# Output projection of a hybrid decoder layer as seven block products of half size

## The chip, the cores and the metric

The kernel runs on one core of a Trainium2 chip. The metric is the device time of one execution in microseconds (us). Five engines matter: TensorE (PE), which multiplies; VectorE (DVE) and ScalarE (ACT), which do the element-wise work; GpSimd (POOL), which does almost nothing here; and SyncE (SP), which issues the transfers from memory. Each works through its own queue in order, and a semaphore makes an instruction wait for one on another engine. Matrix products accumulate in PSUM, in banks of 128 x 512 fp32 numbers.

## What is computed

One decoder layer on 512 tokens of width 1024. The part that the change touches:

```
mixed = sigmoid(gate_a) * y_a + sigmoid(gate_b) * y_b     # [512, 1024]
x = x + mixed @ w_out                                     # w_out [1024, 1024]
h = rmsnorm(x, g_ffn)
x = x + (silu(h @ w1) * (h @ w3)) @ w2
```

Before it stand the two token mixers and their projections (y_a, y_b), after it the feed-forward block (FFN), a gated embedding and a last norm. Results are wanted in fp32.

## The kernel before

**Products in three parts.** Every operand of a large product is split into two fp32r numbers, hi and lo: `split` (L74 to L76) casts hi on ACT (L75) and subtracts on DVE to get lo (L76). `mm3` (L88 to L92) then issues three matmuls, hi by hi (L90), and the two mixed ones (L91, L92). The operand that stands in the array takes a weight load, the other streams its columns: 512 of them for a full bank. Below, "a pass" is one DVE instruction over a 128 x 1024 tile.

**w_out.** Mixed comes transposed, features on partitions, as eight k-tiles `mxh`, `mxl` (L816), made in a loop over four pairs b (L817 to L835): two gate products in PSUM (c), a multiplication into the tile GT (L832), a sum (L834), a split (L835). `down_norm` and `down` (L857 to L907) multiply it with w_out: for each of 8 k-tiles, 4 token tiles t and 2 output halves n, one `mm3` into one of eight accumulators that stand in all eight PSUM banks. That is 8 x 4 x 2 x 3 = 192 matmuls of 512 columns. The tokens stand in the array and the rows of w_out stream. Those rows are loaded by `unit` (L284) in the order of the list `order` (L281), 512 KB each, and split by `wunit` (L78). The last three k-tiles (TAIL = 3) go accumulator by accumulator, so that each bank can be read into the residual `xs` (L882, 8 reads of 512 columns) while the next still accumulates.

**Norm.** With both halves of a token tile in `xs`, `norm` (L123 to L133) squares and sums on ACT (L127), scales on DVE (L129), takes the power on POOL (L130) and multiplies on DVE in two halves (L132). `norm_b` (L913) transposes the result on PE (L920, eight 128-column transposes for a token tile) and splits it into `hhi` and `hlo`. Token tiles 0 and 1 are transposed between the last w_out matmuls; then the FFN begins with `proj_b` (`mm<-hhi,w`, 256 columns), and tiles 2 and 3 follow inside it. Its first weights are the split tile `w10`, made by the hook `load_w1`.

**Order.** PE takes its instructions in the order in which the code is written (L304). For the other engines a scheduler lays out one queue each; what stands in them is quoted below from the built programs.

Of the kernel before, what the change touches and what calls it, by code (L numbers as in the profile page):

```python
# [38 lines left out]
def kernel(  # L39
# [139 lines left out]
    for i, (half, src) in ((0, (0, pT)), (1, (0, wpl)), (0, (1, pT)), (2, (0, wpl)), (1, (1, wpl)), (2, (1, wpl))):  # L179
        raw, hi, lo = ups[i]  # L180
# [97 lines left out]
    for b in range(4):  # L278
        for br in range(2):
            order += [wf[28 + 8 * br + 2 * b], wf[28 + 8 * br + 2 * b + 1], wbr[br, b]]  # L280
    order += [wout[k * P:(k + 1) * P, :] for k in range(KC)]  # L281
    loaded = []

    def unit(ahead=2):  # L284
# [523 lines left out]
    def b16(dt, name):  # L808
        return bp.tile([P, 8, T], dt, tag="b16", name=name, bufs=4)
# [118 lines left out]
    def load_w1(k):

        if k == KC - 4:  # L930
            w = b16(F32R, "w10").rearrange("p (u s k) c -> p u s (k c)", u=2, s=2)
            ws.extend(wunit(w1[f], w[:, f, 0], w[:, f, 1]) for f in range(2))
# [42 lines left out]
    wcount = [0]

    def wtile():
        wcount[0] += 1
        if wcount[0] % 5 < 3:
            return [ring.tile([P, 1024], F32R, tag=tg, name=tg) for tg in ("whi", "wlo")]  # L980
        return [bp.tile([P, 1024], F32R, tag=tg, name=tg, bufs=2) for tg in ("g2h", "g2l")]
# [267 lines left out]
```

## Time and profile before

| | us |
|---|---|
| median of 3 runs | 819.32 (819.28 to 820.4) |
| the profiled execution | 821.62 |
| its span in the trace | 819.8 |
| PE busy | 807.1 (98%) |
| DVE busy | 534.4 (65%) |
| first w_out matmul starts | 372.67 |
| first FFN matmul starts | 418.08 |

The profiled execution is 1.82 us longer than its span (what lies ahead of and behind it), and 2.3 us above the median. Starts are counted from the start of the span. A matmul's listed length includes the time until its result is in the bank; matmuls overlap, so the distance of two starts says what one costs the engine. The same holds for DVE.

### The profile page before, as it was taken

The numbers are of one execution on the slowest core, as the hardware profiler recorded it, in microseconds if no ns is written. First come the engines' busy times: TensorE is split into PE (matmuls) and PEld (weight loads), VectorE is DVE, ScalarE is ACT, GpSimd is POOL, SyncE is SP. The second block draws the span as 40 slices with busy tenths as digits, with TensorE's granted clock in tenths as the row PEclk, the third lists the DMA queues.
The fourth block names the chain that finished last, engine by engine and source line by source line (L and its number), as shares of the span: only waits on it lengthen the run. The fifth ranks groups of instructions, "written<-read, shape, count | busy, mean of one in ns | idle before, by whom it ended". The sixth has DMA issues, their size and how long they took to land.

```text
span 819.8 us, 12525 instructions
## 1 busy us (share of the span) xinstructions
PE 807.1 (98%) x4996; PEld 714.5 (87%) x4996; DVE 534.4 (65%) x879; ACT 365.7 (45%) x679; POOL 42.3 (5%) x67
## 2 busy tenths in 40 slices
PE   8999999999999999999999999999999999999996
PEld 6798888888788888888899999999999988888885
DVE  4878699847673334423489998888887433446654
ACT  6557434435552322322366555555555333434332
POOL 2021100111200000000000000000000000000000
PEclk8999999999999999999999999999999999999999
DMA  8434333211035332233441323333334522443121
GB/s 333 164 97 138 104 101 102 83 52 52 28 108 200 103 102 89 92 103 103 158 163 48 135 92 104 105 109 108 108 111 149 213 84 98 145 163 103 40 89 53
DMA packets 35803, 92.82 MB, mean 113 GB/s; under 512 B 7448, under 2 KB 12184, under 8 KB 35744
## 3 DMA queue, kind: packets, MB, share of 16 engines
q1 hardware_dynamic: 35744, 92.02, 34.3%
q8 instruction: 39, 0.64, 0.3%
q14 instruction: 20, 0.16, 0.1%
HBM read 85.17 MB, written 6.83 MB: 112 GB/s over the span
## 4 chain that ended last, share of the span: by engine, by line
PE 92%; DVE 2%; issue 1%; ACT 1%; POOL 1%; POOLq 0%; DVEq 0%; ACTq 0%
PE c L90 17%; PE c L92 17%; PE c L91 17%; PE mm L90 11%; PE mm L91 11%; PE mm L92 11%; PE c L270 3%; PE pc L90 1%; PE pc L91 1%; PE pc L92 1%; PE c L274 1%; PE c L920 0%; ACT scr L756 0%; POOL fm L120 0%; DVE r L610 0%
## 5 line engine op out<-in xcount | busy, mean ns | idle before, releaser
L76 DVE TENSOR_TENSOR wlo<-raw,whi 128x1024 fp32r<-128x1024 f32 (+1 forms) x102 | 121.3, 1191 | 131.0 <-ACT whi L75 130.3
L75 ACT CAST whi<-raw 128x1024 fp32r<-128x1024 f32 (+1 forms) x102 | 104.4, 1026 | 175.6 <-PE mm L91 66.2
L90 PE MATMUL mm<-hhi,whi 128*128 128x512 f32 x320 | 126.8, 396 | 0.0
L92 PE MATMUL mm<-hhi,wlo 128*128 128x512 f32 x320 | 124.8, 390 | 0.0
L91 PE MATMUL mm<-hlo,whi 128*128 128x512 f32 x320 | 124.7, 390 | 0.0
L92 PEld LDWEIGHTS mm<-hhi,wlo 128*128 128x128 f32 x320 | 60.1, 188 | 12.7
L90 PEld LDWEIGHTS mm<-hhi,whi 128*128 128x128 f32 x320 | 60.1, 188 | 11.8
L91 PEld LDWEIGHTS mm<-hlo,whi 128*128 128x128 f32 x320 | 60.2, 188 | 11.7
L90 PE MATMUL c<-whi,g2h 128*128 128x512 f32 x132 | 51.6, 391 | 0.0
L92 PE MATMUL c<-whi,g2l 128*128 128x512 f32 x132 | 51.4, 389 | 0.0
L91 PE MATMUL c<-wlo,g2h 128*128 128x512 f32 x132 | 51.4, 389 | 0.0
L90 PE MATMUL c<-hhi,whi 128*128 128x256 f32 x168 | 47.7, 284 | 0.0
L91 PE MATMUL c<-hlo,whi 128*128 128x256 f32 x168 | 47.5, 283 | 0.0
L92 PE MATMUL c<-hhi,wlo 128*128 128x256 f32 x168 | 47.5, 283 | 0.0
L75 ACT CAST whi<-sv 128x1024 fp32r<-128x1024 f32 x24 | 25.2, 1052 | 32.5 <-PE pc L91 23.6
L130 POOL TENSOR_TENSOR rstd<-rstd,nhalf 128x1 f32<-128x1 f32 x12 | 6.6, 552 | 554.2 <-DVE rstd L129 554.2
L76 DVE TENSOR_TENSOR g2l<-gg,g2h 128x512 fp32r<-128x512 f32 x22 | 15.0, 688 | 28.2 <-ACT g2h L75 28.2
L91 PEld LDWEIGHTS c<-hlo,whi 128*128 128x128 f32 x168 | 32.2, 192 | 0.0
L92 PEld LDWEIGHTS c<-hhi,wlo 128*128 128x128 f32 x168 | 32.2, 192 | 0.0
L90 PEld LDWEIGHTS c<-hhi,whi 128*128 128x128 f32 x168 | 32.2, 192 | 0.0
L76 DVE TENSOR_TENSOR wlo<-sv,whi 128x1024 fp32r<-128x1024 f32 x24 | 29.1, 1220 | 4.4 <-ACT whi L75 4.4
L75 ACT CAST g2h<-gg 128x512 fp32r<-128x512 f32 x22 | 13.5, 617 | 36.2 <-PE c L91 33.8
(387 smaller groups left out, 2136.1 us busy)
## 6 DMA issues: line engine op xcount, KB each, us to landing
raw<-in_w_dram SPq DMA_DIRECT2D x66, 512.0 KB, 3.5
raw<-in_wf_dram SPq DMA_DIRECT2D x44, 512.0 KB, 3.4
raw<-in_wbr_dram SPq DMA_DIRECT2D x8, 512.0 KB, 3.3
raw<-in_wout_dram SPq DMA_DIRECT2D x8, 512.0 KB, 3.4
raw<-in_wpg_dram SPq DMA_DIRECT2D x8, 512.0 KB, 3.5
gm<-in_x_dram SPq DMA_DIRECT2D x4, 512.0 KB, 8.4
gb<-in_gains_dram SPq DMA_DIRECT2D x4, 512.0 KB, 4.7
pp_dram<-GT SPq DMA_DIRECT2D x8, 256.0 KB, 4.9
```

Source lines behind the costliest of these rows:

```text
L75: S.copy(hi, src)
L76: V.tensor_tensor(lo, src, hi.bitcast(F32), ALU.subtract)
L90: PE.matmul(ps, lhsT=ah, rhs=bh, start=first, stop=False, skip_group_check=more)
L91: PE.matmul(ps, lhsT=ah, rhs=bl, start=False, stop=False, skip_group_check=more)
L92: PE.matmul(ps, lhsT=al, rhs=bh, start=False, stop=last, skip_group_check=more)
L130: G.tensor_tensor(r, r, nhalf[:, 0:1], ALU.pow)
L270: PE.matmul(ps, lhsT=lhsT, rhs=rhs, start=start, stop=stop)
L274: PE.transpose(ps, src, ident if idn is None else idn)
```

## The change

mixed (A) and w_out (B) are cut into 2 x 2 blocks. Token tiles 0 and 1 are the upper half of A, tiles 2 and 3 the lower; of each pair of k-tiles the even one belongs to the left half of A (and the upper of B), the odd one to the right (lower); the output's two halves of 512 columns are the left and right half of B. Seven products of blocks, each of 256 tokens by 512 features by 512 columns, replace the eight of the plain way:

```
P1 = A11 B11   P2 = A12 B21   P3 = S1 T1   P4 = S2 T2
P5 = S4 B22    P6 = S3 T3     P7 = A22 T4
S1 = A21 + A22, S2 = S1 - A11, S3 = A11 - A21, S4 = A12 - S2
T1 = B12 - B11, T2 = B22 - T1, T3 = B22 - B12, T4 = B21 - T2
```

Each product is 2 token tiles (tp) x 4 pairs x 3 = 24 matmuls of 512 columns. A's sums are made by DVE on 256 elements inside the loop over b (L883 to L889), and for each factor of a product there is a split of 128 x 1024 (`s12`, `s43`, `a12`, and two of weights). B's sums are DVE passes of 1024 elements (L1021, L1029, L1042, L1043, two each) in tiles `ra` and `rb`, which hold all of w_out unsplit in the space of `hhi` and `hlo`; so these loads (L858, eight of 512 KB) can start only once the branch products before w_out have read `hhi`. B11 and B21 come by loads of their own (L842, eight of 256 KB) into `raw`.

Of the eight banks the products use six: P1, P4, P6, P7 follow each other in one pair (`pa`, c_3509 and c_3510 below), P3 and P5 in another (`pb_`, mm8_3590 and mm8_3591), and P2 has its own. After each product `res` (L1000) adds each of its two banks to one block of `xs` (14 reads instead of 8), and the next product of the same pair adds on top of what the bank holds. Thus the read of a bank must be over before that bank's next product begins. Token tiles 0 and 1 are normed after P5 and transposed after P6's two halves; tiles 2 and 3 are normed after P7. `load_w1` is called ahead of P6.

```diff
-    order += [wout[k * P:(k + 1) * P, :] for k in range(KC)]
...
-            V.tensor_tensor(tg[j], tg[j], tg[2 + j], ALU.add)
-            split(mxh[:, 2 * b + j, :], mxl[:, 2 * b + j, :], tg[j])
+            V.tensor_tensor(mx[:, b, j, :], tg[j], tg[2 + j], ALU.add)
+        split(a12[:, :, 0, b, :], a12[:, :, 1, b, :], mx[:, b, :, lo_t])
+
+        V.tensor_tensor(s1[:, b, :], mx[:, b, 0, hi_t], mx[:, b, 1, hi_t], ALU.add)
...
+        if b == 3:
+            w_out_first()
...
-    xn = down_norm(KC, lambda k: (mxh[:, k, :], mxl[:, k, :]), load_w1, xs, gb, norm_b)
+    def sprod(acc, tp, pa, pb, first, pairs=range(4)):
+        ah, al = pa
+        c = slice(tp * P, tp * P + P)
+        for i in pairs:
+            mm3(acc, ah[:, i, c], al[:, i, c], *pb[i], first and i == 0, i == 3, not first)
+
+    def res(acc, t, n):
+        c = slice(n * 512, (n + 1) * 512)
+        V.scalar_tensor_tensor(xs[:, t, c], acc, 0.5, xs[:, t, c], ALU.mult, ALU.add)
...
+    for u in us:
+        V.tensor_tensor(ra[:, u, 512:], rb[:, u, 512:], ra[:, u, 512:], ALU.subtract)
+        V.tensor_tensor(rb[:, u, 0:512], rb[:, u, 0:512], ra[:, u, 0:512], ALU.subtract)
+    split(*S3, mx[:, :, 0, hi_t])
+    T3 = bparts(lambda u: ra[:, u:u + 2, 512:])
+    xn = []
+    for tp in range(2):
+        sprod(pb_[tp], tp, S4, B22, False)
+        res(pb_[tp], tp, 1)
+        xn.append(norm(xs[:, tp, :], gb))
+    split(*A11, mx[:, :, 1, hi_t])
+    T4 = bparts(lambda u: rb[:, u:u + 2, 0:512])
+    load_w1()
+    for tp in range(2):
+        sprod(pa[tp], tp, S3, T3, False)
+        res(pa[tp], 2 + tp, 1)
+        norm_b(tp, xn[tp])
+    for tp in range(2):
+        sprod(pa[tp], tp, A11, T4, False)
+        res(pa[tp], 2 + tp, 0)
+        xn.append(norm(xs[:, 2 + tp, :], gb))
```

(`split(*A11, ...)` here writes the block A22 into the tile that held A11.)

**DVE, the end of w_out.** Before, in the last stretch DVE reads accumulators (L882), norms, and splits a few weights:

```order
L76 TENSOR_TENSOR w10_3632<-raw_3637,w10_3632 128x1024
L76 TENSOR_TENSOR wlo_3644<-raw_3641,whi_3643 128x1024
L882 SCALAR_TENSOR_TENSOR xs_3464<-c_3474,xs_3464 128x512
L882 SCALAR_TENSOR_TENSOR xs_3464<-c_3475,xs_3464 128x512
L129 TENSOR_SCALAR rstd_3670<-ss_3668 128x1
L882 SCALAR_TENSOR_TENSOR xs_3464<-c_3476,xs_3464 128x512
L132 SCALAR_TENSOR_TENSOR xn_3667<-xs_3464,rstd_3670,gb_3469 128x512 x2
```

After, between the reads of P4's banks and those of P5's (mm8_3590, mm8_3591) there stand seven passes:

```order
L1000 SCALAR_TENSOR_TENSOR xs_3499<-c_3509,xs_3499 128x512
L1000 SCALAR_TENSOR_TENSOR xs_3499<-c_3510,xs_3499 128x512
L1042 TENSOR_TENSOR ra_3489<-rb_3490,ra_3489 128x2x512
L1043 TENSOR_TENSOR rb_3490<-rb_3490,ra_3489 128x2x512
L1042 TENSOR_TENSOR ra_3489<-rb_3490,ra_3489 128x2x512
L1043 TENSOR_TENSOR rb_3490<-rb_3490,ra_3489 128x2x512
L76 TENSOR_TENSOR s43_3618<-mx_2654,s43_3618 128x1024
L76 TENSOR_TENSOR g2l_3662<-ra_3489,g2h_3661 128x1024
L76 TENSOR_TENSOR g2l_3666<-ra_3489,g2h_3665 128x1024
L1000 SCALAR_TENSOR_TENSOR xs_3499<-mm8_3590,xs_3499 128x512
L1000 SCALAR_TENSOR_TENSOR xs_3499<-mm8_3591,xs_3499 128x512
```

And from there to the read of P6's first bank (c_3509, the last row) five more, with the norms of token tiles 0 and 1 between them:

```order
L76 TENSOR_TENSOR a12_2655<-mx_2654,a12_2655 128x1024
L129 TENSOR_SCALAR rstd_3685<-ss_3683 128x1
L76 TENSOR_TENSOR wlo_3714<-rb_3490,whi_3713 128x1024
L132 SCALAR_TENSOR_TENSOR xn_3682<-xs_3499,rstd_3685,gb_3504 128x512 x2
L129 TENSOR_SCALAR rstd_3706<-ss_3704 128x1
L76 TENSOR_TENSOR wlo_3718<-rb_3490,whi_3717 128x1024
L132 SCALAR_TENSOR_TENSOR xn_3703<-xs_3499,rstd_3706,gb_3504 128x512 x2
L76 TENSOR_TENSOR w10_3721<-raw_3722,w10_3721 128x1024
L76 TENSOR_TENSOR w10_3721<-raw_3726,w10_3721 128x1024
L1000 SCALAR_TENSOR_TENSOR xs_3499<-c_3509,xs_3499 128x512
```

What moved: the splits of `w10` now stand directly ahead of the read of P6's first bank, and the norms' multiplications stand behind P7's weight splits.

**PE, the end of w_out.** Before, transposes of normed tiles stand between matmuls of other accumulators:

```order
L91 MATMUL mm8_3478<-wlo_3644,mxh_2654 128x512
L92 MATMUL mm8_3478<-whi_3643,mxl_2655 128x512
L920 MATMUL c_3713<-cst_sb_75,xn_3667 128x128 x4
L90 MATMUL mm8_3479<-whi_3574,mxh_2654 128x512
L91 MATMUL mm8_3479<-wlo_3575,mxh_2654 128x512
```

There the four transposes of one half of tile 0 (xn_3667) come when five accumulators are done. After, tile 0's (xn_3682) stand between P6's two banks:

```order
L91 MATMUL c_3509<-g2l_3666,s43_3618 128x512
L92 MATMUL c_3509<-g2h_3665,s43_3618 128x512
L976 MATMUL c_3743<-cst_sb_75,xn_3682 128x128 x4
L976 MATMUL c_3751<-cst_sb_75,xn_3682 128x128 x4
L90 MATMUL c_3510<-g2h_3661,s43_3618 128x512
```

and tile 1's (xn_3703) between P6's last matmul and P7's first:

```order
L92 MATMUL c_3510<-g2h_3665,s43_3618 128x512
L976 MATMUL c_3772<-cst_sb_75,xn_3703 128x128 x4
L976 MATMUL c_3780<-cst_sb_75,xn_3703 128x128 x4
L90 MATMUL c_3509<-whi_3713,a12_2655 128x512
L91 MATMUL c_3509<-wlo_3714,a12_2655 128x512
```

What moved: the transposes came from between the products of other accumulators to two places with one product on either side, and P7's first matmul goes to the bank (c_3509) that the last DVE row above reads.

## Rows read from the trace of the kernel before

**Rows 1.** The page: busy time, and busy tenths in 40 slices of the span.
```profile
PE 807.1 (98%) x4996; PEld 714.5 (87%) x4996; DVE 534.4 (65%) x879; ACT 365.7 (45%) x679; POOL 42.3 (5%) x67
...
DVE  4878699847673334423489998888887433446654
...
PEclk8999999999999999999999999999999999999999
```

**Rows 2.** Windows: from:to us, length, busy by engine (instructions), PEclk, DMA share, GB/s.
```profile
5.00:10.00 5.00, 3.41 (x8) 1.94 (x9) 3.45 (x5) 2.75 (x6) 0.00 (x0) 0.73 0.95 349
10.00:15.00 5.00, 5.00 (x15) 3.95 (x14) 1.57 (x3) 2.38 (x5) 0.56 (x1) 0.59 1.03 389
...
405.00:415.00 10.00, 10.00 (x50) 8.26 (x49) 7.00 (x12) 4.75 (x9) 1.12 (x2) 1.00 0.33 137
...
435.00:445.00 10.00, 9.86 (x82) 9.69 (x82) 10.00 (x10) 5.57 (x7) 0.00 (x0) 1.00 0.01 2
```

**Rows 3.** Timeline of PE, before and in the w_out stage: start us, length us, instruction.
```profile
367.01 0.39 PE L92 MATMUL mm<-hhi,wlo 128*128 128x512 f32 x1
...
372.67 0.39 PE L90 MATMUL c<-whi,mxh 128*128 128x512 f32 x1
...
373.35 0.39 PE L90 MATMUL c<-whi,mxh 128*128 128x512 f32 x1
...
418.08 0.28 PE L90 MATMUL mm<-hhi,w 128*128 128x256 f32 x1
```

**Rows 4.** Timeline of DVE, the w_out stage and the FFN's start.
```profile
372.87 0.69 DVE L832 SCALAR_TENSOR_TENSOR GT<-GT,c 128x512 f32<-128x512 f32 x1
...
415.18 0.15 DVE L129 TENSOR_SCALAR rstd<-ss 128x1 f32<-128x1 f32 x1 [0.36 <-ACT xn L127]
415.32 0.69 DVE L882 SCALAR_TENSOR_TENSOR xs<-c,xs 128x512 f32<-128x512 f32 x1
415.99 1.41 DVE L132 SCALAR_TENSOR_TENSOR xn<-xs,rstd,gb 128x512 f32<-128x512 f32 x2
417.32 1.28 DVE L76 TENSOR_TENSOR hlo<-c,hhi 128x512 fp32r<-128x512 f32 x2
418.52 0.68 DVE L882 SCALAR_TENSOR_TENSOR xs<-c,xs 128x512 f32<-128x512 f32 x1
419.12 2.35 DVE L76 TENSOR_TENSOR wlo<-raw,whi 128x1024 fp32r<-128x1024 f32 x2
...
431.93 1.21 DVE L76 TENSOR_TENSOR g2l<-raw,g2h 128x1024 fp32r<-128x1024 f32 x1
433.07 1.22 DVE L961 TENSOR_TENSOR hF<-hF 128x1024 f32<-128x1024 f32 x1
```

**Rows 5.** Groups of DVE by shape, 420 to 640 us; and ACT's casts, on the page.
```profile
L1078 DVE TENSOR_TENSOR GT<-pc,GT 128x256 f32<-128x256 f32 x20 | 8.5, 424 | 12.6 <-PE pc L92 12.4
...
L75 ACT CAST whi<-raw 128x1024 fp32r<-128x1024 f32 (+1 forms) x102 | 104.4, 1026 | 175.6 <-PE mm L91 66.2
```

**Rows 6.** DMA issues: line, KB each, us from issue to landing (the page).
```profile
raw<-in_wout_dram SPq DMA_DIRECT2D x8, 512.0 KB, 3.4
...
gm<-in_x_dram SPq DMA_DIRECT2D x4, 512.0 KB, 8.4
```

**Rows 7.** Timeline of PE near the start: [idle before it, and the releaser].
```profile
5.13 0.50 PE L90 MATMUL mm<-whi 128*128 128x512 f32 x1 [0.49 <-ACT whi L75]
...
7.82 0.79 PE L90 MATMUL mm<-whi 128*128 128x512 f32 x1 [1.23 <-ACT whi L75]
...
9.56 0.63 PE L90 MATMUL mm<-whi 128*128 128x512 f32 x1
9.99 0.63 PE L91 MATMUL mm<-wlo,whi 128*128 128x512 f32 x1
...
14.21 0.39 PE L92 MATMUL mm<-whi,wlo 128*128 128x512 f32 x1
```

**Rows 8.** Timeline of PE at 220 us, a wait inside the kernel.
```profile
219.86 0.63 PE L274 MATMUL c<-cst_sb,num 128*128 128x128 f32 x4 [1.34 <-DVE num L759]
```

More of the change, by code (lines that the diff above doesn't have):

```diff
@@ L813, with wtile, halves, bparts @@
         split(gsh[:, i, :], gsl[:, i, :], gm[:, i, :])
-    mxh, mxl = b16(F32R, "mxh"), b16(F32R, "mxl")
+    wcount = [0]
+    def wtile():
+        wcount[0] += 1
+        if wcount[0] % 5 < 3:
+            return [ring.tile([P, 1024], F32R, tag=tg, name=tg) for tg in ("whi", "wlo")]
+        return [bp.tile([P, 1024], F32R, tag=tg, name=tg, bufs=2) for tg in ("g2h", "g2l")]
+    def halves(t):
+        return t.rearrange("p (u c) -> p u c", c=512)
+    def bparts(src):
+        us = []
+        for u in (0, 2):
+            hi, lo = wtile()
+            split(halves(hi), halves(lo), src(u))
+            us += [(hi[:, c:c + 512], lo[:, c:c + 512]) for c in (0, 512)]
+        return us
+    def from_dram(odd):
+        def src(u):
+            raw = ring.tile([P, 1024], F32, tag="raw", name="raw")
+            for i in range(2):
+                k = 2 * (u + i) + odd
+                nc.sync.dma_start(raw[:, 512 * i:512 * i + 512], wout[k * P:(k + 1) * P, 0:512])
+            return halves(raw)
+        return src
+    bw = {}
+    def w_out_first():
+        wcount[0] = 2
+        bw["B11"] = bparts(from_dram(0))
+        bw["B21"] = bparts(from_dram(1))
+        for n, tg in (("ra", "hhi"), ("rb", "hlo")):
+            bw[n] = hp.tile([P, 4, D], F32, tag=tg, name=n)
+        for n in ("ra", "rb"):
+            for i in range(4):
+                k = 2 * i + (n == "rb")
+                nc.sync.dma_start(bw[n][:, i, :], wout[k * P:(k + 1) * P, :])
+    mx = b16(F32, "mx").rearrange("p (b j) t -> p b j t", j=2)
+    a12 = b16(F32R, "a12").rearrange("p a b -> p (a b)").rearrange("p (j s b t) -> p j s b t", j=2, s=2, t=256)
+    s1 = xnp.tile([P, D], F32, tag="xn", name="s1").rearrange("p (b t) -> p b t", t=256)
+    lo_t, hi_t = slice(0, 256), slice(256, 512)
     for b in range(4):
@@ L833 @@
         for j in range(2):
-            V.tensor_tensor(tg[j], tg[j], tg[2 + j], ALU.add)
-            split(mxh[:, 2 * b + j, :], mxl[:, 2 * b + j, :], tg[j])
+            V.tensor_tensor(mx[:, b, j, :], tg[j], tg[2 + j], ALU.add)
+        split(a12[:, :, 0, b, :], a12[:, :, 1, b, :], mx[:, b, :, lo_t])
+        V.tensor_tensor(s1[:, b, :], mx[:, b, 0, hi_t], mx[:, b, 1, hi_t], ALU.add)
+        V.tensor_tensor(mx[:, b, 0, hi_t], mx[:, b, 0, lo_t], mx[:, b, 0, hi_t], ALU.subtract)
+        V.tensor_tensor(mx[:, b, 0, lo_t], s1[:, b, :], mx[:, b, 0, lo_t], ALU.subtract)
+        V.tensor_tensor(mx[:, b, 1, lo_t], mx[:, b, 1, lo_t], mx[:, b, 0, lo_t], ALU.subtract)
+        if b == 3:
+            w_out_first()
     banks = [0]
@@ L926, with load_w1 @@
     ws = []
[L928 to L932, printed above, removed]
-    xn = down_norm(KC, lambda k: (mxh[:, k, :], mxl[:, k, :]), load_w1, xs, gb, norm_b)
+    def load_w1():
+        w = b16(F32R, "w10").rearrange("p (u s k) c -> p u s (k c)", u=2, s=2)
+        ws.extend(wunit(w1[f], w[:, f, 0], w[:, f, 1]) for f in range(2))
+    def sprod(acc, tp, pa, pb, first, pairs=range(4)):
[3 more added lines that the diff above has]
+            mm3(acc, ah[:, i, c], al[:, i, c], *pb[i], first and i == 0, i == 3, not first)
@@ new lines, in res, with parts4, b16s @@
+    def res(acc, t, n):
+        c = slice(n * 512, (n + 1) * 512)
+        V.scalar_tensor_tensor(xs[:, t, c], acc, 0.5, xs[:, t, c], ALU.mult, ALU.add)
+    def parts4(t, i):
+        return t[:, i, 0], t[:, i, 1]
+    def b16s(name):
+        t = b16(F32R, name).rearrange("p a b -> p (a b)").rearrange("p (j s b t) -> p j s b t", j=2, s=2, t=256)
+        return parts4(t, 0), parts4(t, 1)
+    ra, rb = bw["ra"], bw["rb"]
+    A11, A12 = parts4(a12, 0), parts4(a12, 1)
+    pa = [mm8() for _ in range(2)]
@@ new lines @@
+    for pairs in ((0, 1, 2), (3,)):
+        for tp in range(2):
+            sprod(pa[tp], tp, A11, bw["B11"], True, pairs)
+    for tp in range(2):
+        res(pa[tp], tp, 0)
+    S1, S2 = b16s("s12")
+    split(*S1, s1)
+    us = [slice(u, u + 2) for u in (0, 2)]
+    for u in us:
+        V.tensor_tensor(ra[:, u, 0:512], ra[:, u, 512:], ra[:, u, 0:512], ALU.subtract)
+    T1 = bparts(lambda u: ra[:, u:u + 2, 0:512])
+    pc = [mm8() for _ in range(2)]
+    for tp in range(2):
+        sprod(pc[tp], tp, A12, bw["B21"], True)
+        res(pc[tp], tp, 0)
@@ new lines @@
+    split(*S2, mx[:, :, 0, lo_t])
+    for u in us:
+        V.tensor_tensor(ra[:, u, 0:512], rb[:, u, 512:], ra[:, u, 0:512], ALU.subtract)
+    T2 = bparts(lambda u: ra[:, u:u + 2, 0:512])
+    pb_ = [mm8() for _ in range(2)]
+    for tp in range(2):
+        sprod(pb_[tp], tp, S1, T1, True)
+        res(pb_[tp], 2 + tp, 1)
+    S4, S3 = b16s("s43")
+    split(*S4, mx[:, :, 1, lo_t])
+    B22 = bparts(lambda u: rb[:, u:u + 2, 512:])
+    for tp in range(2):
+        sprod(pa[tp], tp, S2, T2, False)
+        res(pa[tp], tp, 1)
@@ new lines @@
+    for u in us:
+        V.tensor_tensor(ra[:, u, 512:], rb[:, u, 512:], ra[:, u, 512:], ALU.subtract)
[3 more added lines that the diff above has]
+    xn = []
+    for tp in range(2):
+        sprod(pb_[tp], tp, S4, B22, False)
[3 more added lines that the diff above has]
+    T4 = bparts(lambda u: rb[:, u:u + 2, 0:512])
@@ L937 @@
+    load_w1()
+    for tp in range(2):
+        sprod(pa[tp], tp, S3, T3, False)
+        res(pa[tp], 2 + tp, 1)
+        norm_b(tp, xn[tp])
+    for tp in range(2):
+        sprod(pa[tp], tp, A11, T4, False)
+        res(pa[tp], 2 + tp, 0)
+        xn.append(norm(xs[:, 2 + tp, :], gb))
     order += [w3[0], w3[1]]
@@ L974 @@
     raws, parts_ = {}, {}
[L975 to L981, printed above, removed]
+    wcount[0] = 0
     def p_load(j):
```

## Prediction

> **What bounds the kernel now.** The page comes first: PE is busy for 98% of the span and runs at full clock after the first slices, DVE for 65% with much room in the middle [rows 1]. So time comes from PE, and another engine can only take some away. Next the windows of the w_out stage: from 405 to 415 us PE is busy all the time, DVE for 7.00 of 10 us and ACT for 4.75; a little later, from 435 to 445, DVE is busy for the whole 10.00 and PE waits 0.14 [rows 2]. That says two things: nothing holds PE back in w_out, and DVE is not far from being the bound in this part of the kernel. Last, the timelines: the first w_out matmul starts at 372.67, the first FFN matmul at 418.08, which makes the stage 45.41 us long; the first three matmuls, one mm3, take 0.68, hence 0.2267 for one [rows 3]. The 192 matmuls are 43.5 of it, the 16 transposes and their borders the other 1.9.
>
> **What PE saves.** Seven products of 24 matmuls are 168, which is 24 fewer: 24 x 0.2267 = 5.44 us. The 16 transposes stay. Left alone, PE would begin the FFN at 412.6 instead of 418.08.
>
> **What DVE gets.** The path that decides runs over DVE, and I add it up from its own row. The last gate product lands in PSUM and DVE multiplies it at 372.87 [rows 4]; this does not move, since the gate matmuls before it are the same. From there the order after has, up to and including the read of P6's first bank, these instructions, counted row by row:
>
> 25 passes over 1024 elements: 8 sums of weights (L1021, L1029, L1042, L1043), 10 splits of weights (T1, T2, B22, T3 and T4, two each), 5 splits of A's factors (s12 and s43 two each, a12 one), 2 splits of w10. Two of the same kind take 2.35, and from one to the next it is 1.14 (431.93 to 433.07) [rows 4]. 25 x 1.14 = 28.50.
>
> 13 instructions of 512 elements: the gate product itself, one sum, one split, and 10 reads of banks. A read of a bank is followed by the next instruction after 0.60 (418.52 to 419.12) [rows 4]. 13 x 0.60 = 7.80. A 14th, the read of P6's first bank, counts in full: 0.69.
>
> 4 small sums of 256 elements: their length is 0.42 [rows 5]; the next starts 0.08 before the end, as with the others, so 0.34 each, 1.36.
>
> Two norms: 0.14 for the scaling (415.18 to 415.32), 1.33 for the two multiplications (415.99 to 417.32) [rows 4], together 2.94.
>
> The sum is 41.29, so the read ends at 372.87 + 41.29 = 414.16. P7's first matmul adds to the bank just read and cannot start before. A matmul after a wait shows 0.50 against 0.39 [rows 7], so I add 0.11. P7 is 24 x 0.2267 = 5.44, and the FFN begins at 419.71: **1.63 us later than before**. In other words PE could stand at P7 at 407.2, waits 7.0 for DVE in all, and has 5.44 to pay for it.
>
> Does DVE really run without a gap? At each place where it waits for PE I compared both sums. Reading P2's second bank comes at 384.7 by DVE's sum; PE has it at 383.7. P3's banks are read at 387.6 and 390.5; PE has them at 386.4 and 389.2. P4's second bank comes at 395.1, with PE done at 394.9: the closest place, and a wait of a few tenths there would go straight into the result. P5's follow four sums and three splits later, when PE has long stopped.
>
> **Where PE waits.** P6's first matmul with a lo part needs the 19th pass: 402.6 by DVE's sum, 400.1 by PE's. That is 2.5 (P4 may take some tenths of it). Next, the transposes of tile 0 need the first half of xn, which stands behind a split of T3, two reads, the split of A22 and one of T4: 408.0, against PE at 405.1, so 2.9. P7's wait is the rest, about 1.4, since P6's second half and tile 1's transposes fill 408.7 to 412.7. The two w10 splits were spread out before; now they stand right ahead of the read that P7 waits for, and cost 2.28 of the sum.
>
> **What I cost at nothing.** ACT's casts: each is 1.03 [rows 5], shorter than the DVE pass of the same tile; the stage has about 25 of them, some 26 us in 41, and ACT was busy 4.75 in 10 [rows 2]. If a cast is late, DVE stops and the sum grows by as much. The loads: 8 x 256 KB come early, while the branch products run. The 8 x 512 KB wait for the last reader of hhi, which starts at 367.01 and is done at 367.4 [rows 3]. The first sum of weights wants rows 0 and 2 of them, second and third in the queue, at 374.07. One load of 512 KB takes 3.4 [rows 6]; further ones at 389 GB/s [rows 2] 1.35 each: 367.5 + 3.4 + 2.7 = 373.6, so 0.5 to spare. The first read of a bank moves up by the whole stage, and the banks are free, since six of eight are used. Sums that read what the instruction before wrote may wait for its end: 5 such places at 0.08, 0 to 0.4; I take 0. Behind w_out, reads and norms of tiles 2 and 3 stand where they stood; at most the 0.14 of PE's wait at 435 to 445 comes back.
>
> **A rule on DVE against the rows.** In the timeline the next instruction starts 0.08 before the listed end of a pass of 1.22, even where the two have nothing in common (431.93, 433.07) [rows 4]. The Trainium skill, page "VectorE: DVE Perf Modes", section "The DRAIN you can't avoid", says that the next op does not start until the pipe is empty. If so, each instruction costs its listed length. The trace disagrees by these 0.08.
>
> **The rivals.** The base case is the sum: 819.32 + 1.63 = 820.95, so 821.0. The profiled execution of before would become 823.2, as it lies 2.3 above the median.
>
> (a) *The clock falls.* Near the start PE waited 0.49 and 1.23 with three matmuls between; then the windows show a granted clock of 0.73 and 0.59, and a matmul took 0.43 (9.56 to 9.99) until 14.2, that is for 6.4 us [rows 2, 7]. Full speed is 2.4 GHz, the low level 1.2. Against it: a single wait of 1.34 at 219.86 [rows 8] left the clock alone [rows 1]. Here there are 2.5 and 2.9 with one half product between, more than either. If the clock falls behind the second wait, 12 matmuls take 0.20 more each, 2.4, and the transposes about 0.9, less the 1.4 that P7 waits anyway: +1.9. If it has fallen before and recovers by then: 0. If it falls behind the third wait: 15 matmuls of P7, +3.0. I take +1.5: 822.5, with 0 to 3.0.
>
> (b) *The weights come late.* Four loads of 512 KB issued together took 8.4 in the middle [rows 6]. If the third needs that, it lands at 375.9, and everything on DVE shifts by 1.8: 822.8. For it: the queue holds eight such loads. Against it: they have the memory nearly to themselves.
>
> (c) *DVE is not the bound.* If its chain is short enough, because sums and splits on strided halves take less than the rows I took, or overlap more, the 24 matmuls show: 819.32 - 5.44 = 813.9. It decides at a chain of 39.7 us for no change and at about 34.3 for the whole gain. Passes would have to cost 0.93 instead of 1.14; no row of DVE over 1024 fp32 elements in these groups is under 1.21. That fewer matmuls are issued than the change says is excluded by the order: 168 are in it.
>
> (d) *Each DVE instruction costs its listed length.* 25 x 1.22 + 14 x 0.68 + 4 x 0.42 + 2 x 1.41 + 2 x 0.15 = 44.8, which is 3.5 more: 824.5. This would be the rule named above; the rows speak against it.
>
> **How the numbers follow.** Base 0.49, its own range 820.4 to 821.8; (a) 0.33; (b) 0.09; (c) 0.06; (d) 0.03. A measurement of this kernel tells about 0.2%, 1.6 us, from no change, so "same" is 817.7 to 820.96. The base lies on that border; its unknown costs are more often above it than below, so I give 0.22 of it to same and 0.27 to slower. Of (a) and (b) 0.04 end where the extra cost is near nothing and come to same, the rest is slower. (c) is 0.06 faster. Together: faster 0.06, same 0.26, slower 0.68. The range leaves out (c), (d) and the upper end of (a): 819.8 to 823.8.
>
> **What would show it.** Right: DVE without idle from 373 to 414 us; three waits of PE, at P6, at the transposes of tile 0 and at P7, all put down to DVE, of 2.5, 2.9 and 1.4; the FFN's first matmul at 419.7; 4972 matmuls. Wrong: PE busy through the stage (then (c)); matmuls 0.43 apart and a clock below 1.00 between 402 and 420 (then (a)); DVE waiting at its first sum of weights for a transfer (then (b)); passes 1.22 apart (then (d)).

## The result, and the profile after

| | before | after |
|---|---|---|
| median of 4 runs, us | 819.86 (819.28 to 820.79) | 825.22 (824.75 to 825.71) |
| ratio, 95% interval | | 1.0065 (1.005 to 1.008) |
| the profiled execution / its span, us | 821.62 / 819.8 | 825.05 / 823.3 |

The change makes the kernel 5.4 us slower, 0.65%. The direction was forecast, the size was not: 825.22 lies above the range. The page of after, busy time and the slices that answer to [rows 1]:

```profile
PE 803.1 (98%) x4972; PEld 710.5 (86%) x4972; DVE 562.6 (68%) x916; ACT 374.2 (45%) x686; POOL 44.4 (5%) x67
...
PE   8999999999999999999799999999999999999996
...
DVE  4868798857663533449999998888887433445654
```

The 24 matmuls are gone (4972 in place of 4996) and PE is busy 4.0 us less, yet the span is longer. DVE, at 3 and 4 tenths in the two slices of w_out before (the 19th and 20th, 370 to 411 us), is at 9 in both, and PE has a slice of 7 there. The window that answers to 405 to 415 in [rows 2]:

```profile
405.00:415.00 10.00, 6.69 (x30) 5.71 (x31) 9.10 (x14) 3.20 (x6) 2.94 (x2) 0.83 0.34 122
```

PE is busy 6.69 of 10 us, at a granted clock of 0.83; DVE 9.10. POOL's two instructions take 2.94, as against 1.12 before: this was not foreseen at all.

Where the time went, from the starts of four matmuls in both timelines (first of w_out, first of the FFN, first on pc, first transpose of the norm behind the FFN) and the span:

| stretch, us | before | after | |
|---|---|---|---|
| start to w_out | 372.67 | 371.42 | -1.25 |
| w_out to FFN | 45.41 | 48.68 | +3.27 |
| FFN to pc | 26.63 | 26.84 | +0.21 |
| pc to the transposes | 314.23 | 315.44 | +1.21 |
| from there to the end | 60.9 | 60.9 | 0 |

The first line is not the change's: near the start the clock stood at 0.84 and 0.82 in this execution, at 0.73 and 0.59 in that of before [rows 2], and it differs from one execution to the next (w_out began between 370.1 and 373.0 in the traces of this study). Without it the traces differ by 4.7 us, which agrees with the ratio's interval (4.1 to 6.6 us). So **3.3 us were lost in w_out, where 1.6 were forecast, and 1.4 behind it, where nothing was**.

The w_out stage in PE's timeline: the first matmul, the three waits, and the FFN's first matmul.

```profile
371.42 0.39 PE L90 MATMUL c<-g2h,a 128*128 128x512 f32 x1
...
402.05 0.50 PE L91 MATMUL c<-g2l,s 128*128 128x512 f32 x1 [1.97 <-DVE g2l L76]
...
408.01 1.94 PE L976 MATMUL c<-cst_sb,xn 128*128 128x128 f32 x8 [3.17 <-DVE xn L132]
409.60 0.78 PE L90 MATMUL c<-g2h,s 128*128 128x512 f32 x1
410.17 0.63 PE L91 MATMUL c<-g2l,s 128*128 128x512 f32 x1
410.60 0.63 PE L92 MATMUL c<-g2h,s 128*128 128x512 f32 x1
...
414.51 0.50 PE L90 MATMUL c<-whi,a 128*128 128x512 f32 x1 [0.30 <-DVE xs L1000]
...
420.10 0.28 PE L90 MATMUL c<-hhi,w 128*128 128x256 f32 x1
```

The waits stand where they were expected, at P6, at tile 0's transposes and at P7, and all on DVE; two small ones come before them, 0.25 us at P3 and 0.23 at P4. Behind the second of the three the clock is at its low level of 1.2 GHz (granted clock 0.50 from 408 to 410 us): eight transposes take 1.59 us to the next start (0.79 at full clock before), and 410.17 to 410.60 is 0.43 for one matmul. DVE's side, from the last gate product on (the first six rows), the two norms, and the read that P7 waits for:

```profile
371.69 0.69 DVE L881 SCALAR_TENSOR_TENSOR GT<-GT,c 128x512 f32<-128x512 f32 x1 [1.38 <-PE c L92]
372.41 0.69 DVE L883 TENSOR_TENSOR mx<-GT 128x512 f32<-128x512 f32 x1
373.27 1.23 DVE L1021 TENSOR_TENSOR ra<-ra 128x1024 f32<-128x1024 f32 x1 [0.17 <-DMA ra<-in_wout_dram]
...
375.02 0.42 DVE L886 TENSOR_TENSOR s<-mx 128x256 f32<-128x256 f32 x1
375.47 0.42 DVE L887 TENSOR_TENSOR mx<-mx 128x256 f32<-128x256 f32 x1
376.02 1.23 DVE L76 TENSOR_TENSOR wlo<-ra,whi 128x1024 fp32r<-128x1024 f32 x1
...
405.39 0.14 DVE L129 TENSOR_SCALAR rstd<-ss 128x1 f32<-128x1 f32 x1
405.45 1.21 DVE L76 TENSOR_TENSOR wlo<-rb,whi 128x1024 fp32r<-128x1024 f32 x1
407.11 1.42 DVE L132 SCALAR_TENSOR_TENSOR xn<-xs,rstd,gb 128x512 f32<-128x512 f32 x2 [0.45 <-POOL rstd L130]
...
413.78 0.68 DVE L1000 SCALAR_TENSOR_TENSOR xs<-c,xs 128x512 f32<-128x512 f32 x1
```

From 371.69 to the end of the read at 414.46 it is 42.77 us, where the sum had 41.29. P7 starts 0.05 later. The pass at 376.02 starts when ACT's cast of the same tile ends:

```profile
374.93 1.05 ACT L75 CAST whi<-ra 128x1024 fp32r<-128x1024 f32 x1 [1.17 <-DVE ra L1021]
```

### The profile page after: what moved, and what is told of

It reads as the page before. It is cut to its first block, busy times and chain, and to the rows that moved or that the text cites. A ratio compares the mean times of both kernels' runs of the same rounds, so it can differ in the third digit from the quotient of the medians.

```text
span 823.3 us, 12553 instructions
## 1 busy us (share of the span) xinstructions
PE 803.1 (98%) x4972; PEld 710.5 (86%) x4972; DVE 562.6 (68%) x916; ACT 374.2 (45%) x686; POOL 44.4 (5%) x67
## 4 chain that ended last, share of the span: by engine, by line
PE 81%; DVE 9%; issue 3%; DMA 2%; ACT 2%; POOL 1%; SPq 0%; POOLq 0%; DVEq 0%; ACTq 0%
PE c L90 14%; PE c L91 14%; PE c L92 14%; PE mm L90 10%; PE mm L91 10%; PE mm L92 10%; PE c L270 2%; DVE wlo L76 1%; PE pc L90 1%; PE pc L92 1%; PE pc L91 1%; PE c L274 1%; DVE xs L1000 1%; DVE g2l L76 1%; DMA ra<-in_wout_dram 1%
## 5 line engine op out<-in xcount | busy, mean ns | idle before, releaser
L76 DVE TENSOR_TENSOR wlo<-raw,whi 128x1024 fp32r<-128x1024 f32 (+1 forms) x96 | 114.0, 1189 | 108.0 <-ACT whi L75 107.3
L75 ACT CAST whi<-raw 128x1024 fp32r<-128x1024 f32 (+1 forms) x96 | 98.1, 1024 | 166.6 <-PE mm L91 65.3
L90 PE MATMUL mm<-hhi,whi 128*128 128x512 f32 (+1 forms) x344 | 133.7, 389 | 0.0
L92 PE MATMUL mm<-hhi,wlo 128*128 128x512 f32 (+1 forms) x344 | 131.5, 382 | 0.0
L91 PE MATMUL mm<-hlo,whi 128*128 128x512 f32 (+1 forms) x344 | 131.4, 382 | 0.0
L90 PE MATMUL c<-hhi,whi 128*128 128x256 f32 x144 | 40.8, 283 | 0.0
L91 PE MATMUL c<-hlo,whi 128*128 128x256 f32 x144 | 40.8, 283 | 0.0
L92 PE MATMUL c<-hhi,wlo 128*128 128x256 f32 x144 | 40.7, 283 | 0.0
L92 PEld LDWEIGHTS c<-whi,g2l 128*128 128x128 f32 x132 | 24.8, 188 | 5.2
L90 PEld LDWEIGHTS c<-whi,g2h 128*128 128x128 f32 x132 | 24.8, 188 | 5.1
L91 PEld LDWEIGHTS c<-wlo,g2h 128*128 128x128 f32 x132 | 24.8, 188 | 4.9
```

## The experiments

Each kernel ran in turn with the kernel before on the same chip; a ratio is to that kernel. "Stage" is the stretch from the first w_out to the first FFN matmul, in the one execution that was profiled. Beside the changed kernel the kernel before took 819.86 us, beside e1, e3, e4 and e5 820.33, beside e6 to e9 820.54 and beside e10 to e12 820.53, so that times of different groups can differ by up to 0.7 us for that alone.

### Is it VectorE's chain? The sums left out, and the sums on GpSimd

e3_no_sums leaves the eight sums of weight blocks out, so that its output is another one:

```diff
-    for u in us:
-        V.tensor_tensor(ra[:, u, 0:512], ra[:, u, 512:], ra[:, u, 0:512], ALU.subtract)
...
-        V.tensor_tensor(rb[:, u, 0:512], rb[:, u, 0:512], ra[:, u, 0:512], ALU.subtract)
```

> The changed kernel without the eight sums of weight blocks (T1 to T4 are then plain blocks of w_out): eight VectorE passes of 1.14 us, 9.1 us, leave the chain, all else stays. Theory A (VectorE's chain of 42.8 us sets the end of w_out): the chain is 33.7 us and TensorE becomes the bound; waits inside w_out fall under 1 us, the FFN starts 48.7 - 7 = 41 us after the first w_out matmul, and the time is 5 to 8 us under the changed kernel, 817 to 820. Rival C (the clock that fell at 408 us, or the reading of banks, is what costs): waits at the norm stay, gain under 3 us, 822 or more.

Measured: 816.54 us, ratio 0.9953 (0.994 to 0.9967); stage 40.64 us (370.93 to 411.57). One wait of 0.4 is left in it. Its windows in the stage's second half:

```profile
391.00:401.00 10.00, 10.00 (x46) 8.28 (x45) 9.93 (x13) 7.86 (x9) 0.56 (x1) 1.00 0.30 106
401.00:411.00 10.00, 10.00 (x54) 8.40 (x53) 8.51 (x13) 5.45 (x12) 1.47 (x1) 1.00 0.43 134
```

PE is busy all the time. With 9.1 us off DVE's chain the stage is 8.0 shorter, and the 24 matmuls show: 40.64 is near the 40.0 that 168 matmuls and the transposes need. So the chain holds w_out back. (The time fell a little more than expected, by 8.7. In the traces 8.0 of it lie in the stage and 0.3 behind it; the rest is in the start, which differs from one execution to the next.)

e4_pool_sums gives the same eight sums to GpSimd:

```diff
-        V.tensor_tensor(ra[:, u, 0:512], ra[:, u, 512:], ra[:, u, 0:512], ALU.subtract)
+        G.tensor_tensor(ra[:, u, 0:512], ra[:, u, 512:], ra[:, u, 0:512], ALU.subtract)
...
```

> The changed kernel with the eight sums of weight blocks on GpSimd in place of VectorE; the computation is the whole one. GpSimd does almost nothing in this stage. Theory A: VectorE's chain is 9.1 us shorter; if GpSimd takes 2 to 2.5 us for a sum and does not slow VectorE, its 8 sums are 16 to 20 us beside 40, and the stage gains as without the sums, 817 to 820, at or under the kernel before. If both engines hold each other up (a GpSimd sum far over 2.5 us, or VectorE passes over 1.3 us), part of it comes back: 821 to 826. Rival C (clock or bank reads): gain under 3 us.

Measured: 832.24 us, ratio 1.0142 (1.012 to 1.0163); stage 56.98 us. Worse than even the bad case. POOL's timeline, then DVE's at the same place:

```profile
386.60 3.27 POOL L1043 TENSOR_TENSOR rb<-rb,ra 128x1024 f32<-128x1024 f32 x1
389.82 3.38 POOL L1029 TENSOR_TENSOR ra<-rb,ra 128x1024 f32<-128x1024 f32 x1
```

```profile
388.13 2.83 DVE L76 TENSOR_TENSOR s<-mx,s 128x1024 fp32r<-128x1024 f32 x1
390.88 3.40 DVE L76 TENSOR_TENSOR g2l<-ra,g2h 128x1024 fp32r<-128x1024 f32 x1
```

Beside a sum of 3.4 us on POOL a DVE pass takes 2.8 to 3.4 in place of 1.2: the two engines hold each other up. The ends show that they take turns: POOL's sum ends at 389.87, DVE's pass 1.09 later (390.96), POOL's next sum 2.24 behind that (393.20) and DVE's next pass 1.08 behind that (394.28). The Trainium skill, page "SBUF — State Buffer", section "SBUF: two separate sides", says that DVE and GpSimd share a pair of ports as an exclusive lock, taken for a whole instruction by whichever starts first, where the DVE op has two SBUF inputs and the GpSimd op reads SBUF. The rows agree.

The same thing, small, is in the changed kernel. POOL's power for the norm, in after beside a DVE pass with two SBUF inputs (405.45 above), and in before beside a DVE read of PSUM (415.32 in [rows 4]):

```profile
405.61 1.47 POOL L130 TENSOR_TENSOR rstd<-rstd,nhalf 128x1 f32<-128x1 f32 x1 [177.89 <-DVE rstd L129]
```

```profile
415.41 0.55 POOL L130 TENSOR_TENSOR rstd<-rstd,nhalf 128x1 f32<-128x1 f32 x1 [4.47 <-DVE rstd L129]
```

It is one number per partition and takes 1.47 us; DVE then stands 0.45 for it, at both norms.

### What does the fallen clock cost? Filled waits, and w10 out of the way

e5_fill puts 21 matmuls, whose results nobody reads, into the two long waits:

```diff
+    fill(8, S4, B22)
     for tp in range(2):
         sprod(pa[tp], tp, S3, T3, False)
+        if tp == 0:
+            fill(13, S3, T3)
```

> The changed kernel with 21 matmuls more on a bank that nobody reads any longer: 8 (1.8 us) ahead of P6, where TensorE waits 2.0 us, and 13 (2.9 us) ahead of the transposes of tile 0, where it waits 3.2 us. They fill the waits and keep TensorE at work. Theory A (VectorE's chain ends last; the clock that fell costs only what TensorE would else have waited at P7): the clock stays at 1.00, the wait at P7 grows from 0.3 to 1.3 us or more, and the time moves by less than 0.5 us, 824.7 to 825.7. Rival C (the fallen clock costs): 1.5 to 2.5 us faster, 822.7 to 823.7.

Measured: 823.95 us, ratio 1.0042 (1.003 to 1.0055). The clock stayed at 1.00. In PE's timeline the wait at P7 is 1.64, as theory A has it, but in DVE's the first sum waits for its load:

```profile
415.69 0.50 PE L90 MATMUL c<-whi,a 128*128 128x512 f32 x1 [1.64 <-DVE xs L1000]
```

```profile
374.45 1.23 DVE L1021 TENSOR_TENSOR ra<-ra 128x1024 f32<-128x1024 f32 x1 [0.98 <-DMA ra<-in_wout_dram]
```

So the stage is 49.46, 0.8 longer, as that wait is in the chain, and the clock gave nothing. e1_banks (below) shows the same without a late load. Its w_out is that of the changed kernel, but in its trace the clock fell behind the first wait, the 1.98 us at P6, and was up again before the second:

```profile
404.00:406.00 2.00, 2.00 (x6) 1.58 (x5) 2.00 (x4) 1.20 (x3) 0.00 (x0) 0.50 0.19 80
```

```profile
409.04 1.23 PE L976 MATMUL c<-cst_sb,xn 128*128 128x128 f32 x8 [1.58 <-DVE xn L132]
...
415.54 0.50 PE L90 MATMUL c<-whi,a 128*128 128x512 f32 x1 [1.64 <-DVE xs L1000]
```

The stage is 48.67 there and 48.68 in after, with 1.64 and 0.30 us of wait at P7. Thus the place at which the clock falls differs between two executions of the same w_out, and as long as DVE's chain ends last it moves only the waits.

That e5 as a whole was 1.3 us faster than the changed kernel was expected by neither theory: from pc to the transposes behind the FFN it took 313.88 in place of 315.44. That led to the fetch, below.

e6_w10_late calls load_w1 behind P6; e7_late_fill does the same and fills the waits as e5 does:

```diff
-    load_w1()
     for tp in range(2):
         sprod(pa[tp], tp, S3, T3, False)
         res(pa[tp], 2 + tp, 1)
         norm_b(tp, xn[tp])
+    load_w1()
```

> The changed kernel with the call of load_w1 behind P6 in place of ahead of it: the two splits of w10, 2.28 us, no longer stand on VectorE ahead of the read that P7 waits for. Theory A (VectorE's chain ends last at P7, but only 0.3 us behind TensorE, which ran P6's second half and tile 0's transposes at the low clock): the wait at P7 goes, the stage from the first w_out matmul to the first FFN matmul shrinks by 0.3 to 0.5 us only, from 48.7 to 48.2 or 48.4; time 824.4 to 825.2. Rival D (the chain alone counts, the clock costs nothing): the stage shrinks by the 1.4 us that TensorE should have had to spare, to 47.3 or less; time 823.5 to 824.

> The run before this with the 21 filling matmuls of e5 as well, so that the clock doesn't fall. Theory A: now TensorE reaches P7 1.5 to 2 us earlier and nothing holds it there: stage 46.6 to 47.2 us, time 822.5 to 823.5, while each of the two edits alone gives under 0.5 us in the stage. Rival D: no further gain over the run before.

Measured: e6 824.68 us, 1.0052 (1.0036 to 1.0067), stage 48.31; e7 822.05 us, 1.0024 (1.0014 to 1.0035), stage 46.82. Tile 0's transposes and P7's first matmul on PE, e6 and then e7:

```profile
408.69 1.72 PE L976 MATMUL c<-cst_sb,xn 128*128 128x128 f32 x8 [3.12 <-DVE xn L132]
...
414.77 0.47 PE L90 MATMUL c<-whi,a 128*128 128x512 f32 x1
```

```profile
408.23 1.23 PE L976 MATMUL c<-cst_sb,xn 128*128 128x128 f32 x8 [0.21 <-DVE xn L132]
...
412.84 0.47 PE L90 MATMUL c<-whi,a 128*128 128x512 f32 x1
```

Nothing waits at P7 in either. Between the two rows it is 6.08 us with the low clock and 4.61 without: 1.5 us. Alone, neither the 2.28 us off the chain nor the clock is worth 0.4 in the stage; together they are worth 1.9, as theory A had it. The two were nearly level, and each hid the other. Not all of it is kept: from FFN to pc it is 27.46 and 27.65 us in place of 26.84, as the wait ahead of pc grows from 0.48 to 1.1 and 1.3. And e7's time of 822.05, under the 822.5 of its expectation, holds 0.9 us that are not the clock's: from pc to the transposes it takes 314.27, e6 315.19 (the fetch, below). The stages are from one trace each, and e1 shows that the place where the clock falls varies.

### What was lost behind w_out? Banks

e1_banks moves the counter of the banks in the changed kernel; e8_before_banks moves it in the kernel before, to where the change leaves it (there the added line is `banks[0] += 6`):

```diff
+    banks[0] += 2
     hps = [mm8() for _ in range(4)]
```

> The changed kernel with one line more: the counter that deals out PSUM banks is moved by two before the FFN's first four accumulators, so that they stand in the same kinds of bank as in the kernel before. Nothing of w_out changes. Theory A (the slower time has two sources: VectorE's chain inside w_out, 3.3 us in the trace, and something after it that comes from the shifted banks and late transfers, about 2 us): the wait of 0.5 us before the matmul on pc at 458 us goes; 0.4 to 0.6 us faster than the changed kernel, 824.6 to 824.8. If the late read of the last accumulators near 760 us hangs on the banks too, 2 us faster, 823.2. Rival B (all of it comes from w_out): no change, 825.2.

> The kernel before, whole, with one line more: the counter of the PSUM banks is moved by six ahead of the FFN's first accumulators, which then stand as in the changed kernel; w_out is untouched. Theory A (part of the loss is behind w_out and comes from this shift): a wait of 0.5 us or more before the first matmul on pc; 0.4 to 1.2 us slower than the kernel before. On the late load near 755 us: if the shift makes it, the wait for the last split of w_ple_gate rises from 1.2 to over 2.5 us here too, and 1 to 1.5 us more are lost; if that load is late by chance or through w_out's change, it is as before. Rival B (the shift costs nothing): as the kernel before, within 0.3 us.

Measured: e1 824.83 us, 1.0049 (1.0036 to 1.0062); from FFN to pc 26.20 in place of 26.84, with no wait left. e8 821.51 us, 1.0009 (0.9999 to 1.0018); stage 45.41 as before, and from FFN to pc 27.82 in place of 26.63. The first matmul on pc, in after and in e8:

```profile
446.94 0.36 PE L90 MATMUL pc<-hhi,whi 128*128 128x256 f32 x1 [0.48 <-DVE gg L1164]
```

```profile
443.75 0.36 PE L90 MATMUL pc<-hhi,whi 128*128 128x256 f32 x1 [1.35 <-DVE gg L1044]
```

w_out took twelve banks in turn before it came to the FFN's four, and takes ten now. So the FFN's last two accumulators, which are read last, stand where pc comes next, and pc waits. In the traces this costs 0.6 us in the changed kernel and 1.2 in the kernel before; the times alone (ratio up to 1.0018) don't settle it. (The wait stands at 446.94 in after, not at 458 as e1's expectation has it.) That more of the loss hung on the banks (the late read at 760 us) fell: e1 keeps it, its cast waits 3.25 us, and in e8 the cast waits 1.25, as in before.

### What was lost behind w_out? A fetch of instructions

PE's wait at the transposes behind the FFN in after (before has none there), and the cast on ACT behind the last load of w_ple_gate, in after and in before:

```profile
PE c L140 <- DVE xn L132: 1.5, 1, 1.5
```

```profile
758.38 1.05 ACT L75 CAST wqh<-raw 128x1024 fp32r<-128x1024 f32 x1 [3.80 <-DMA raw<-in_wpg_dram]
```

```profile
754.28 1.06 ACT L75 CAST wqh<-raw 128x1024 fp32r<-128x1024 f32 x1 [1.21 <-DMA raw<-in_wpg_dram]
```

That load comes late; its split stands ahead of the reads and norms of that stage on DVE. DMA in after while it runs (753.1 to 758.4 us): GB/s in 40 slices, then the queues' packets; below it the same of before (751 to 754.4).

```profile
GB/s 0 0 0 0 0 0 0 247 62 31 371 185 371 340 340 278 495 402 433 186 62 31 0 31 0 0 31 0 0 31 31 31 31 0 31 31 0 0 0 0
...
q1 hardware_dynamic: 146, 0.52, 29.8%
q8 instruction: 1, 0.02, 1.1%
```

```profile
q1 hardware_dynamic: 152, 0.54, 49.8%
```

In after a packet of an instruction queue lies inside the load, which then trails off in single small packets for two microseconds. In before there is none. Of the first ten traces of this study six had that packet inside the load (all with PE's stream shortened by the 24 matmuls: after, e1, e3, e4, e6, e9), and there the cast waits 2.7 to 3.8 us; in the other four (before, e8, e5, e7) it lies ahead, and the wait is 1.2 to 1.4. The queue follows PE's stream: its 39 packets of an execution come one for about 255 of PE's instructions, and the one in question comes when PE has started 9368 to 9391 of them, in every trace (of DVE's it is 1022 in before and 1071 in after). e5 and e7 are the kernels with 21 matmuls added. e10_pad tests it: the changed kernel with 21 small matmuls in P6's wait alone.

```diff
+    fill(21, S4, B22, 64)
     for tp in range(2):
         sprod(pa[tp], tp, S3, T3, False)
```

> The changed kernel with 21 small matmuls more (64 columns each, on a bank nobody reads any longer), all in the 2 us that TensorE waits at P6; w_out's order, its waits and the low clock behind the second wait stay. What they move is the place at which TensorE's next piece of instructions is fetched from memory: in six traces with 24 matmuls fewer and late last splits of w_ple_gate, a packet of the instruction queue lies inside that last load (755.3 us in the changed kernel); in four traces without the lateness it lies 8 to 9 us ahead. Theory F (the fetch holds up one part of the load): the packet moves ahead, the wait for the last load falls from 3.8 to under 1.6 us, the stretch from the first pc matmul to the first transpose behind the FFN shrinks from 315.4 to 314.3 us, while the stage stays at 48.7; time 0.8 to 1.3 us under the changed kernel, 823.9 to 824.4. Rival G (the load is late by chance or for w_out's loads): no change, 825.2.

Measured: 823.85 us, ratio 1.0044 (1.0032 to 1.0057). The stage is 48.62, with the low clock behind the second wait; from pc to the transposes 313.82. The cast, and the queues from 753.9 to 757.4 us:

```profile
757.39 1.05 ACT L75 CAST wqh<-raw 128x1024 fp32r<-128x1024 f32 x1 [1.70 <-DMA raw<-in_wpg_dram]
```

```profile
q1 hardware_dynamic: 149, 0.53, 47.1%
```

The packet lies 8 us ahead of the cast, the load is in time, and 1.4 us are back without a change in what is computed: 1.6 in the traces from pc to the transposes, while the two ratios' intervals still overlap a little. (The wait is 1.70 where under 1.6 was expected.) e11 and e12 below, with 21 matmuls added as well, have the packet 8 us ahead too, and the cast waits 1.47 and 1.21. So the lateness goes with the packet's place in all traces, and matmuls that change nothing else move both. No run moves the packet alone, so that the packet itself holds the load up is the likeliest reading and not shown; how a packet of about 1 us would do it by two is open.

### Can the order be mended?

e9_reorder keeps the whole change and moves what need not stand ahead of P7: norms and w10 behind P6's reads, both tiles' transposes between P7's halves; banks as in e1; ra and rb change places (cut, from two places):

```diff
-        for n, tg in (("ra", "hhi"), ("rb", "hlo")):
+        for n, tg in (("ra", "hlo"), ("rb", "hhi")):
...
+    for tp in range(2):
+        xn.append(norm(xs[:, tp, :], gb))
+    load_w1()
     for tp in range(2):
         sprod(pa[tp], tp, A11, T4, False)
+        if tp == 0:
+            for i in range(2):
+                norm_b(i, xn[i])
```

> The whole change, with its order mended at four places: the norms of tiles 0 and 1 and the splits of w10 come behind P6's reads on VectorE, and the transposes of both tiles between P7's two halves, so that no product waits for a norm; ra stands in the space of hlo and rb in that of hhi, so that ra's loads are first; banks as in e1. Theory A (VectorE's work of 42 us is too much, but a good part of it need not stand ahead of P7): P7 starts after about 36.5 us of VectorE's chain in place of 42.8; waits at P6 (2 us) and P7 (about 1 us) stay; stage 43 to 45.5 us against 48.7 and 45.4 before; time 817.5 to 820.5, that is at or just under the kernel before. Rival E (VectorE is full anyhow and the work put off returns as waits in the FFN): stage shorter, but from its end to the first pc matmul 1 to 3 us longer; time 821 to 824.

Measured: 821.82 us, ratio 1.0019 (1.0009 to 1.0028); stage 46.82. Neither theory: nothing came back in the FFN (26.20 to pc), but the stage is longer than expected. Two rows of DVE and PE tell why:

```profile
371.81 1.23 DVE L1021 TENSOR_TENSOR ra<-ra 128x1024 f32<-128x1024 f32 x1 [2.29 <-DMA ra<-in_wout_dram]
```

```profile
401.86 0.50 PE L91 MATMUL c<-g2l,s 128*128 128x512 f32 x1 [1.97 <-DVE g2l L76]
...
402.49 0.63 PE L90 MATMUL c<-g2h,s 128*128 128x512 f32 x1
402.92 0.63 PE L91 MATMUL c<-g2l,s 128*128 128x512 f32 x1
```

With ra's loads first, the first sum came to stand ahead of the last gate product, and held the whole queue for 2.29 us. And the clock fell behind one wait of 1.97; nothing waits at P7's start, so the slow matmuls lie in PE's way here. How the excess divides between the two is not shown. Behind pc e9 has the late load too (315.00 us to the transposes, 314.23 in before).

e11_best takes the exchange of ra and rb back and fills P6's wait; e12_best2 also puts T4's sums behind T3's splits, so that the waiting is all at P7, and fills there (the first diff is e11's filling, the second what e12 has in its place):

```diff
+    fill(4, S4, B22)
+    fill(17, S4, B22, 64)
     for tp in range(2):
         sprod(pa[tp], tp, S3, T3, False)
```

```diff
     T3 = bparts(lambda u: ra[:, u:u + 2, 512:])
+    for u in us:
+        V.tensor_tensor(rb[:, u, 0:512], rb[:, u, 0:512], ra[:, u, 0:512], ALU.subtract)
...
+    fill(10, S3, T3)
+    fill(11, S3, T3, 64)
     for tp in range(2):
         sprod(pa[tp], tp, A11, T4, False)
```

> The whole change with the order of e9 (norms of tiles 0 and 1 and w10's splits behind P6's reads, transposes between P7's halves) and the banks of e1, but ra and rb where the change has them, and 21 filling matmuls at P6's wait (4 of 512 columns, 17 of 64) for the clock and the fetch. In e9 the first sum of weights stood ahead of the last gate product and waited 2.3 us for its load; that goes. Theory A: stage 44.5 to 45.8 us, no loss behind it; time 818.5 to 820.5, about the kernel before. Rival E (VectorE full, so that it comes back as waits in the FFN): 821 to 823.

> As the run before, with the sums for T4 (L1043) put behind T3's splits and the filling matmuls (10 of 512 columns, 11 of 64) ahead of P7: VectorE's work is the same, but P6 needs two passes less of it and should not wait, and the waiting is all at P7, about 3 us. Theory A (the chain up to P7 decides, however the waits are cut): stage and time within 0.5 us of the run before. Rival H (waits ahead of P6 cost by themselves, through the clock or the bank reads): 1 us or more faster than the run before.

Measured: e11 820.23 us, ratio 0.9998 (0.9989 to 1.0007), stage 45.64; e12 819.91 us, ratio 0.9996 (0.9987 to 1.0005), stage 45.51. So theory A: how the waits are cut makes no difference, and both are level with the kernel before, not ahead of it. DVE in e12 from 380 to 410 us:

```profile
380.00:390.00 10.00, 9.32 (x40) 7.04 (x39) 10.00 (x12) 5.05 (x5) 0.00 (x0) 1.00 0.00 0
390.00:400.00 10.00, 10.00 (x46) 8.25 (x45) 10.00 (x11) 4.01 (x4) 0.00 (x0) 1.00 0.01 2
400.00:410.00 10.00, 10.00 (x51) 8.46 (x50) 9.55 (x13) 5.14 (x7) 2.06 (x2) 1.00 0.26 105
```

It is full, 29.55 of 30 us (PE's 10.00 holds the filling matmuls). In none of the orders tried could PE's 5.44 us be had; they showed only in e3, where element-wise work was taken out of the stage.

## Why the prediction was wrong, step by step

**What bounds the kernel; PE's saving.** Right. 24 matmuls of 0.2267 us went, and e3 shows them as time once DVE is not in the way.

**DVE's chain sets the end.** Right as a mechanism: P7 starts 0.05 us after the read's end, DVE idles only 1.1 us in listed waits (0.17 and twice 0.45), and e3 shows it by taking work away. Wrong in size: 42.77 us in place of 41.29. The terms of the sum that were too small: the two norms by 0.9, since POOL's power, which the sum leaves out without a reason, takes 1.47 us beside a pass on SBUF and not the 0.55 of before; instructions that did not start 0.08 ahead of the end of the one before, by 0.5; the load by 0.17. The 0.5 are four places: 372.41 and 375.47, which read what the instruction before them wrote or overwrite what it read (0.1 each), 373.27 behind the load (0.1 without its wait), and 376.02, which stood for ACT's cast (0.2). For the first kind a bound of 0 to 0.4 was given and 0 taken; the casts were taken at nothing. The passes themselves were a little cheaper than 1.14. With 0.05 from the read's end to P7, P7 at 5.59 in place of 5.44 + 0.11, and 0.07 at the stage's start this makes +3.27 in place of +1.63.

**The waits.** 2.5, 2.9 and 1.4 were forecast; 2.2 (with P4's), 3.2 and 0.3 came. The third is short because PE itself was late, by the clock; in e1, where the clock was up again by then, they are 2.2, 1.6 and 1.6.

**(a), the clock.** It fell, as the rival has it, behind the second wait; in e1 behind the first, which the rival priced at 0. Its price in the changed kernel was nothing that the traces show, and not 1.5: the stage is 48.68 and 48.67, since PE only used up the wait at P7. The 1.9 that was worked out for this case (3.3 slower less 1.4 of wait) took slow matmuls for half of P6; it was about three. e6 and e7 show 1.5 us once the chain is shorter.

**(b), the late weights.** In small: 0.17 us in after, 0.98 in e5. From the start of hhi's last reader (365.76) to the first sum of weights it was 7.5 us in after and 8.3 in e5, where the sum had 6.6 for the landing, so the margin of 0.5 was too thin to be put at zero. **(c)** and **(d)** fell: DVE is the bound, and two passes still take 2.35 together, not twice their listed 1.22. (c) also has a slip: by its own sum a pass would have to cost 0.86 for the whole gain (28.50 less 7.0, over 25) and 1.08 for no change, not 0.93; and the 1.21 held against it is a listed length, where 1.14 is a distance of starts.

**The steps that failed** are two of about equal size. One is the sum of DVE's chain, too small by 1.5 us of the 1.6 that the stage lost beyond the forecast, the norms' power above all. The stage alone would have kept the time inside the range (819.32 + 3.27 = 822.6); with the other it is 824.0, above it. The other is "behind w_out, reads and norms stand where they stood". Their place is the same, and yet 1.4 us went there in the traces: 0.2 net from the shifted banks (0.6 by e1), which could have been read from the order, as the FFN's accumulators changed from mm to c there; and 1.2 from the late load beside a fetch of instructions, which no view of before shows. The range left out what a moved count can do far from the place of the change.

## What to carry to other kernels

Work taken from the engine that bounds is worth only what the next engine has to spare in that stage: add that engine's work up from the stage's first forced moment, include the waits for small helpers on a third engine, and treat two chains that end within a microsecond of each other as both deciding. When an edit changes how many accumulators or instructions come before a later stage, look at what rotates by count: the bank that each later tile gets, and perhaps where instruction fetches fall against loads that something waits for.

## What was not expected of the hardware

- An instruction packet of 0.02 MB inside a load of 512 KB went with a landing some 2 us later; 21 small matmuls, placed 350 us earlier in a wait, moved it out of the way and gave 1.4 us. That the one causes the other is not shown.
- A GpSimd power on one number per partition took 1.47 us beside a DVE pass with two SBUF inputs, and 0.55 beside one that reads PSUM; sums of 128 x 1024 on GpSimd took 2.4 to 3.4 us and slowed DVE's passes beside them to 2.5 to 3.4.
- The clock stayed up through a wait of 1.97 us in the changed kernel and fell behind one of 1.98 us in e1, whose w_out is the same, and behind one of 1.97 in e9. So the order of the work doesn't settle it; what does, the traces don't tell.
